# Two-block network in one kernel: in block 1 both row tiles of the third attention are finished ahead of the fourth's, with output products between them

## The chip, the cores and the metric

The kernel runs on one core of a Trainium2 chip. The metric is the device time of one execution in microseconds (us), as the median of several runs. TensorE (PE) does matrix products and transposes, VectorE (DVE) and ScalarE (ACT) work on the elements, GpSimd (POOL) does a few powers, SyncE (SP) issues the loads of the weights.

## The reference

Two different blocks of two layers each work on 256 rows of 1024 columns in float32. The change is in block 1. One of its layers, cut to what matters:

```
def hybrid_layer(x, ...):                       # x: 256 rows x 1024
    proj = rmsnorm(x, g_pre_mix) @ w_in         # all inputs of four attentions
    o_a = dsa_attention(...)                    # columns   0..255 of mix
    o_b = forgetting_attention(...)             # columns 256..511
    o_c = differential_attention(...)           # columns 512..767: softmax(q1 k1) - lam * softmax(q2 k2),
                                                #   times v, then an rmsnorm over each head
    o_d = sliding_window_sink_attention(...)    # columns 768..1023
    mix = jnp.concatenate([o_a, o_b, o_c, o_d], axis=-1)
    x = x + rmsnorm(mix @ w_out, g_post_mix)    # the output product
    m = jnp.square(jax.nn.relu(rmsnorm(x, g_pre_mlp) @ w_up)) @ w_down
    x = x + rmsnorm(m, g_post_mlp)
    return x + jax.nn.sigmoid(x @ w_ple_gate) * (p_i @ w_ple_proj)
```

Each attention has four heads of 64 columns, and all are causal. The differential attention has two softmaxes per head, so eight in a row tile.

## The kernel before, in words

The 256 rows are two row tiles of 128, t = 0 and 1. Row 0's tile sees 128 keys, tile 1 sees 256, so tile 1's attention is about twice the work. A float32 product is done as three products of rounded halves (hi and lo), for accuracy.

`layer1` writes one layer of block 1. The projections come first. The attentions are generators (`att_a`, `att_b`, `differ` for the third, `att_d` for the fourth; one per row tile for the last two, `gen_c` and `gen_d`) that are put in the list `self.side`. Long runs of products call `tick` after every few matmuls; a tick advances the first two generators of the list by one step. `until` and `drain` tick on until the named generators, or all, are done. Thus the work of the attentions is written between the products. A scheduler then orders the instructions of each engine, near the order in which they are written; each engine runs its own list in order and waits at the head of it.

One softmax goes through four engines (`soft`, `pv`): PE makes the scores of a head (line 386), DVE adds the mask and takes the maximum (387), ACT takes the exponential with its sum (398); for the third attention DVE divides by the sums and subtracts (555 to 560); PE transposes the result (411), ACT copies it from the bank (413), PE multiplies by the values (419). The third attention ends with its norm: ACT copies and squares (568, 569), DVE sums (571), POOL takes the power (225), DVE scales twice (573, 574).

The output product `mix @ w_out` needs `mix` transposed: `transpose_in` transposes columns of one row tile (249) and splits them into hi and lo (ACT 230, DVE 231) in `mT`. `mT` has eight k-tiles of 128 columns: 0 to 3 are the first two attentions, 4 and 5 the third, 6 and 7 the fourth. `mm_pair` (284) then does, per row tile and k-tile, three terms for each half of the 1024 output columns, six matmuls of 512 columns; 96 in a layer. `pss[t]` are the banks in which they add up. `norm(t)` then squares them (347), scales (798 to 802) and transposes the outcome (249) for the MLP, whose first products are line 268 and, from line 325 on, the wide ones.

Before the change the list is sorted so that tile 0 of the third and of the fourth attention go first, side by side, and then tile 1 of both. The columns 512 to 1023 of a tile are transposed at once, four k-tiles in a row.

Of the kernel before, what the change touches and what calls it, by code (L numbers as in the profile page):

```python
# [21 lines left out]
NT = S // P  # L22
# [107 lines left out]
class Net:  # L130
# [448 lines left out]
    def layer1(self, i, xT):  # L579
# [47 lines left out]
        def q_alone(q, rows=64):  # L627

            qT = [wk.tile([P, 2, 2, P], F32, name="qT", tag="qT") for _ in range(64 // rows)]
            self.tr_alone(lambda r: qT[r // 2][:, r % 2], q, 2, rows)  # L630
            return qT
# [10 lines left out]
        mix = [wk.tile([P, D], F32, name="mix", tag="mix") for _ in range(NT)]  # L642
# [89 lines left out]
        mT = self.new_parts(KT)  # L732
# [8 lines left out]
        gen_c = [self.differ(i, t, lambda t: q_alone(cq[t], 32), kTc, vc, mix[t]) for t in range(NT)]  # L741
# [14 lines left out]
        get = self.w.rows(a["w_out"][i], 0, KT)  # L756
        pss = [[self.bank(self.acc) for _ in range(2)] for _ in range(NT)]
# [5 lines left out]
        def att_d(t):  # L763
            yield from self.attend(t, qTd, kTd, vd, lambda h: h // 2, lambda h: self.window[:, S - (t + 1) * P:],
                                   mix[t][:, 768:1024], self.sink[:, i, :])

        gen_d = [att_d(t) for t in range(NT)]
# [5 lines left out]
        gboth = self.row(a["norm_post_mix"][i])  # L773
        self.pin(nc.vector.tensor_tensor(gboth, gboth, gmlp, op=ALU.mult))
        self.transpose_in(mix[1][:, :512], mT, 1, 4)
        self.side.sort(key=lambda gen: gen in (gen_c[1], gen_d[1]))
        self.mm_pair(pss[0], mT, 0, range(1, 4), get, start=False, stop=False)
        self.until(gen_c[0], gen_d[0])
        self.transpose_in(mix[0][:, 512:], mT, 0, 4, 4)
        self.mm_pair(pss[0], mT, 0, range(4, 6), get, start=False, stop=False)  # L780
        self.mm_pair(pss[1], mT, 1, range(2), get, stop=False)
        self.mm_pair(pss[0], mT, 0, range(6, 8), get, start=False, apart=2)
        xg = []

# [8 lines left out]
        def norm(t):  # L793
            ss = self.square_sum(pss[t])
            u = wk.tile([P, D], F32, name="u", tag="w4")
            for j in range(2):
                sl = slice(j * 512, (j + 1) * 512)
                nc.vector.tensor_tensor(u[:, sl], pss[t][j], gboth[:, sl], op=ALU.mult)
            r = self.rsqrt(self.total(ss), 1.0 / D, EPS)
            for j in range(2):  # L800
                sl = slice(j * 512, (j + 1) * 512)
                nc.vector.scalar_tensor_tensor(xg[t][:, sl], u[:, sl], r, xg[t][:, sl], op0=ALU.mult, op1=ALU.add)
                self.transpose_in(xg[t][:, sl], hT, t, 4, 4 * j)
            us[t], rs[t] = u, r
# [7 lines left out]
            self.pin(nc.vector.tensor_tensor(X[t], X[t], u, op=ALU.add))  # L812

        us, rs = [None] * NT, [None] * NT
        self.mm_pair(pss[1], mT, 1, range(2, 4), get, start=False, stop=False)
        self.drain()
        self.transpose_in(mix[1][:, 512:], mT, 1, 4, 4)
        self.mm_pair(pss[1], mT, 1, range(4, 6), get, start=False, stop=False)
        norm(0)
        self.mm_pair(pss[1], mT, 1, range(6, 8), get, start=False, apart=2)  # L820
        gain(1)
        gpost = self.row(a["norm_post_mix"][i])
# [51 lines left out]
        for f in range(NG - 2):  # L874
            cur = up(f + 1)
            get = self.w.rows(a["w_mlp_down"][i], f * 4, 4)
# [13 lines left out]
        get = self.w.rows(a["w_mlp_down"][i], 4 * NG - 8, 8)  # L890
# [33 lines left out]
        get = self.w.rows(a["w_ple_gate"][i], 0, KT)  # L924
# [4 lines left out]
        pss = [[self.bank(self.acc) for _ in range(2)] for _ in range(NT)]  # L929
# [572 lines left out]
```

## Time and profile before

| what | value |
|---|---|
| median of 3 runs | 1939.16 us (1939.14 to 1940.99) |
| the profiled execution's own time | 1937.16 us |
| its span in the trace | 1935.4 us |
| mean granted TensorE clock | 0.988 of full speed |
| PE busy | 1877.3 us, 97% of the span |
| DVE busy | 1306.8 us, 68% |
| ACT busy | 1035.9 us, 54% |

A matmul in the trace has its modelled end, which overlaps the next one's start; how long one holds PE is read from start to start. Float32 products that aren't split in hi and lo (scores, products with the values) stand as two records each. The granted clock is 1.00 at 2.4 GHz and 0.50 at 1.2 GHz. A row of the windows gives the stretch, its length, the busy time (and instructions) of PE, of its weight loads, of DVE, ACT and POOL, then the granted clock, the busy share of the DMA engines and GB/s.

### The profile page before, as it was taken

The page shows a single profiled execution, that of the slowest core. Times are in us where ns is not written, and L with a number is a line of the kernel's source. Part 1 is how long each engine was busy: PE and PEld are TensorE (multiplying, and loading weights), DVE is VectorE, ACT ScalarE, POOL GpSimd, SP SyncE. Part 2 cuts the span into 40 slices and gives each one's busy share as a digit, 9 for nine tenths or more (in the row PEclk, how much of TensorE's full clock was granted, in tenths as well). Part 3 has the DMA queues.
Part 4 walks back from the last instruction along what each step waited for, and adds up shares of the span by engine and source line. Part 5 has one row for each costly group of instructions (what it writes and reads, how often), then busy time and mean ns, then how long its engine had stood idle before and what let it go on. Part 6 is the DMA issues. An engine that isn't in the chain of part 4 may idle for free.

```text
span 1935.4 us, 27780 instructions
## 1 busy us (share of the span) xinstructions
PE 1877.3 (97%) x10282; PEld 1614.0 (83%) x10282; DVE 1306.8 (68%) x2456; ACT 1035.9 (54%) x1743; POOL 77.8 (4%) x127
## 2 busy tenths in 40 slices
PE   7898999999989999999999999999999999999997
PEld 6787878887878888888888988887988888988886
DVE  6866756687776666558666667566558666677555
ACT  5555544564654545566555655554565555655552
POOL 2000000000000000100000000000000000000000
PEclk9998999999999999999999999999999999999999
DMA  7433676554335555655555656664454555656662
GB/s 214 131 112 97 209 241 210 164 179 133 110 123 186 180 203 158 188 162 162 176 179 181 221 174 211 195 186 141 155 170 155 182 182 172 206 168 217 186 193 89
DMA packets 187132, 334.00 MB, mean 173 GB/s; under 512 B 11622, under 2 KB 109078, under 8 KB 186612
## 3 DMA queue, kind: packets, MB, share of 16 engines
q1 hardware_dynamic: 180160, 308.94, 50.4%
q0 software_dynamic: 6528, 23.18, 3.9%
q8 instruction: 81, 1.33, 0.3%
q14 instruction: 55, 0.45, 0.1%
q10 hardware_dynamic: 308, 0.10, 0.0%
HBM read 331.10 MB, written 4.62 MB: 173 GB/s over the span
## 4 chain that ended last, share of the span: by engine, by line
PE 83%; DVE 7%; DMA 4%; ACT 4%; issue 2%; POOL 0%; DVEq 0%; SPq 0%; ACTq 0%; POOLq 0%
PE bank L325 23%; PE bank L284 20%; PE bank L268 13%; PE bank L327 12%; DMA wraw<-in_w_in_dram 3%; DVE wlo L103 2%; PE bank L386 2%; PE bank L419 2%; PE bank L315 2%; PE bank L314 2%; PE bank L313 2%; ACT whi L102 1%; PE bank L249 1%; ACT pr L398 1%; PE bank L411 1%
## 5 line engine op out<-in xcount | busy, mean ns | idle before, releaser
L103 DVE TENSOR_TENSOR wlo<-wraw,whi 128x1024 fp32r<-128x1024 f32 (+1 forms) x628 | 711.0, 1147 | 328.7 <-ACT whi L102 238.6
L102 ACT ACTIVATE whi<-wraw 128x1024 fp32r<-128x1024 f32 (+1 forms) x628 | 608.9, 997 | 346.1 <-PE bank L284 110.2
L325 PE MATMUL bank<-phl,whi 128*128 128x512 f32 x2080 | 532.3, 395 | 0.4 <-ACT whi L102 0.4
L325 PEld LDWEIGHTS bank<-phl,whi 128*128 128x128 f32 x2080 | 374.9, 189 | 69.1 <-ACT whi L102 1.2
L284 PE MATMUL bank<-whi,phl 128*128 128x512 f32 x1280 | 358.2, 395 | 1.7 <-ACT phl L230 1.0
L268 PE MATMUL bank<-whi,phl 128*128 128x512 f32 (+4 forms) x1152 | 341.2, 378 | 4.3 <-ACT whi L102 2.2
L327 PEld LDWEIGHTS bank<-phl,wlo 128*128 128x128 f32 x2080 | 284.2, 190 | 23.2 <-DVE wlo L103 2.7
L327 PE MATMUL bank<-phl,wlo 128*128 128x256 f32 x2080 | 291.8, 283 | 0.6 <-DVE wlo L103 0.6
L284 PEld LDWEIGHTS bank<-whi,phl 128*128 128x128 f32 x1280 | 237.4, 189 | 53.3 <-ACT phl L230 2.9
L268 PEld LDWEIGHTS bank<-whi,phl 128*128 128x128 f32 x1152 | 210.9, 191 | 34.9 <-ACT phl L230 3.8
L268 PE MATMUL bank<-wlo,phl 128*128 128x512 f32 (+4 forms) x576 | 215.4, 376 | 2.4 <-DVE wlo L103 2.3
L284 PE MATMUL bank<-wlo,phl 128*128 128x512 f32 x640 | 206.2, 394 | 0.1
L284 PEld LDWEIGHTS bank<-wlo,phl 128*128 128x128 f32 x640 | 120.2, 188 | 28.8 <-DVE wlo L103 2.8
L268 PEld LDWEIGHTS bank<-wlo,phl 128*128 128x128 f32 x576 | 110.0, 191 | 18.2 <-DVE wlo L103 4.3
L315 PE MATMUL bank<-phl,wlo 128*128 128x256 f32 x304 | 86.3, 284 | 0.0
L314 PE MATMUL bank<-phl,whi 128*128 128x256 f32 x304 | 86.1, 283 | 0.0
L225 POOL TENSOR_TENSOR ry<-ry,mhalf 128x1 f32<-128x1 f32 (+1 forms) x40 | 32.9, 824 | 1309.1 <-DVE ry L224 1301.6
L313 PE MATMUL bank<-phl,whi 128*128 128x256 f32 x304 | 85.5, 281 | 0.0
L313 PEld LDWEIGHTS bank<-phl,whi 128*128 128x128 f32 x304 | 57.7, 190 | 0.2
L314 PEld LDWEIGHTS bank<-phl,whi 128*128 128x128 f32 x304 | 57.3, 189 | 0.2
L315 PEld LDWEIGHTS bank<-phl,wlo 128*128 128x128 f32 x304 | 57.5, 189 | 0.0
L230 ACT ACTIVATE phl<-bank 128x512 fp32r<-128x512 f32 (+2 forms) x60 | 32.8, 571 | 44.0 <-PE bank L249 43.6
(301 smaller groups left out, 1720.9 us busy)
## 6 DMA issues: line engine op xcount, KB each, us to landing
wraw<-in_w_in_dram SPq DMA_DIRECT2D x172, 512.0 KB, 4.6
wraw<-in_w_mlp_up_dram SPq DMA_DIRECT2D x64, 512.0 KB, 4.6
wraw<-in_w_mlp_down_dram SPq DMA_DIRECT2D x64, 512.0 KB, 4.5
wraw<-in_w_ffn_gate_dram SPq DMA_DIRECT2D x44, 512.0 KB, 4.7
wraw<-in_w_ffn_up_dram SPq DMA_DIRECT2D x44, 512.0 KB, 4.5
wraw<-in_w_ffn_down_dram SPq DMA_DIRECT2D x44, 512.0 KB, 4.4
wraw<-in_w_in_dram SPq DMA_DIRECT2D x54, 384.0 KB, 3.8
wraw<-in_w_out_dram SPq DMA_DIRECT2D x32, 512.0 KB, 4.3
```

The costliest lines, as they stand in the source:

```text
L102: first = nc.scalar.activation(hi[:, :n], src, AF.Copy)
L103: ins = nc.vector.tensor_tensor(lo[:, :n], src, hi[:, :n].bitcast(F32), op=ALU.subtract)
L225: nc.gpsimd.tensor_tensor(y, y, self.mhalf[:, :n], op=ALU.pow)
L268: self.order(nc.tensor.matmul(ps, self.part(parts, kt)[x][:, sl], get(kt + kbase)[w], start=start and n == 0, stop=stop and n == len(terms ...
L284: ins = nc.tensor.matmul(pss[j], self.part(parts, kt)[x][:, sl], get(kt + kbase)[w][:, j * 512:(j + 1) * 512], start=start and n == 0, sto ...
L313: self.order(nc.tensor.matmul(ps, wh, xh, start=first, stop=False, **kw), n == 0)
L314: nc.tensor.matmul(ps, wh, xl, start=False, stop=False, **kw)
L315: nc.tensor.matmul(ps, wl, xh, start=False, stop=last, **kw)
L325: self.order(nc.tensor.matmul(flat, get(kt)[0][:, c:c + P], both, start=n == 0, stop=False), n == 0)
L327: nc.tensor.matmul(ps[:, 0], get(kt)[1][:, c:c + P], self.part(parts, kt)[0], start=False, stop=n == len(kts) - 1)
L386: nc.tensor.matmul(o, qs(h), ks(h), start=True, stop=True)
L419: nc.tensor.matmul(po[:, h * 64:(h + 1) * 64], pts[kb][:, h, :], v(kb, h), start=kb == 0, stop=kb == t)
```

## The change

In `layer1`, the sort of the list is left out, so the third attention's two tiles are advanced together first, and the fourth's after them. The transposes into `mT` go by two k-tiles: the third attention's for both row tiles once both are done, then the fourth's for tile 0, then for tile 1. The products of k-tiles 0 and 1 of tile 1 are written ahead of the wait for the third attention, those of 4 and 5 of tile 0 and of 2 and 3 of tile 1 behind it. `norm(0)` is written ahead of tile 1's last four k-tiles.

```
-        self.side.sort(key=lambda gen: gen in (gen_c[1], gen_d[1]))
         self.mm_pair(pss[0], mT, 0, range(1, 4), get, start=False, stop=False)
-        self.until(gen_c[0], gen_d[0])
-        self.transpose_in(mix[0][:, 512:], mT, 0, 4, 4)
+        self.mm_pair(pss[1], mT, 1, range(2), get, stop=False)
+        self.until(*gen_c)
+        for t in range(NT):
+            self.transpose_in(mix[t][:, 512:768], mT, t, 2, 4)
         self.mm_pair(pss[0], mT, 0, range(4, 6), get, start=False, stop=False)
-        self.mm_pair(pss[1], mT, 1, range(2), get, stop=False)
+        self.mm_pair(pss[1], mT, 1, range(2, 4), get, start=False, stop=False)
+        self.until(gen_d[0])
+        self.transpose_in(mix[0][:, 768:], mT, 0, 2, 6)
         self.mm_pair(pss[0], mT, 0, range(6, 8), get, start=False, apart=2)
...
-        self.mm_pair(pss[1], mT, 1, range(2, 4), get, start=False, stop=False)
+        norm(0)
+        self.mm_pair(pss[1], mT, 1, range(4, 6), get, start=False, stop=False)
         self.drain()
-        self.transpose_in(mix[1][:, 512:], mT, 1, 4, 4)
-        self.mm_pair(pss[1], mT, 1, range(4, 6), get, start=False, stop=False)
-        norm(0)
+        self.transpose_in(mix[1][:, 768:], mT, 1, 2, 6)
         self.mm_pair(pss[1], mT, 1, range(6, 8), get, start=False, apart=2)
```

The lists of the built programs show where this puts the work. In the names below, `bank_1460` and `bank_1461` are `pss[0]`, `bank_1462` and `bank_1463` are `pss[1]`; `phl_1024` holds k-tiles 0 to 3 of `mT`, `phl_1025` k-tiles 4 to 7; `mix_165` and `mix_166` are the two row tiles of `mix`. All is in layer 0; layer 1 has the same pattern.

On PE, before, the products of tile 0 with k-tiles 4 to 7 stand among the scores of tile 1 of the third (`kT_1168`) and of the fourth attention (`kT_1470`):

```order
L386 MATMUL bank_1635<-kT_1168,qT_1569 128x256
L284 MATMUL bank_1460<-whi_1438,phl_1025 128x512
L284 MATMUL bank_1461<-whi_1438,phl_1025 128x512
L386 MATMUL bank_1640<-kT_1168,qT_1569 128x256
L386 MATMUL bank_1654<-kT_1470,qT_1481 128x256
L284 MATMUL bank_1460<-whi_1438,phl_1025 128x512
L284 MATMUL bank_1461<-whi_1438,phl_1025 128x512
```

With the change, the first product of k-tiles 4 to 7 on PE stands behind the values' products of tile 1 of the third attention (`pt_1662`) and behind the transposes of the fourth attention's tile 1 (`pr_1667`):

```order
L419 MATMUL bank_1688<-v_1166,pt_1662 128x64
L411 MATMUL bank_1708<-ident_79,pr_1667 128x128
L411 MATMUL bank_1715<-ident_79,pr_1667 128x128
L249 MATMUL bank_1722<-ident_79,mix_165 128x128 x2
L411 MATMUL bank_1708<-ident_79,pr_1667 128x128
L411 MATMUL bank_1715<-ident_79,pr_1667 128x128
L411 MATMUL bank_1708<-ident_79,pr_1667 128x128
L411 MATMUL bank_1715<-ident_79,pr_1667 128x128
L411 MATMUL bank_1708<-ident_79,pr_1667 128x128
L411 MATMUL bank_1715<-ident_79,pr_1667 128x128
L284 MATMUL bank_1460<-whi_1438,phl_1025 128x512
L284 MATMUL bank_1461<-whi_1438,phl_1025 128x512
```

So no output product is left between the scores of tile 1 and this place; the last one ahead of it is of k-tile 3 of tile 1.

The second place is where PE transposes what `norm(0)` made (`xg_1765` before, `xg_1785` now), ahead of the last products of tile 1. Before, the transposes of `mix_166` stand first, and 24 products of `pss[1]` behind:

```order
L419 MATMUL bank_1745<-v_1166,pt_1725 128x64
L249 MATMUL bank_1781<-ident_79,mix_166 128x128 x4
L249 MATMUL bank_1814<-ident_79,xg_1765 128x128 x4
L249 MATMUL bank_1822<-ident_79,xg_1765 128x128 x2
L284 MATMUL bank_1462<-whi_1438,phl_1025 128x512
L284 MATMUL bank_1463<-whi_1438,phl_1025 128x512
```

With the change, five products of `pss[1]` stand between the last product of `pss[0]` (`bank_1461`) and these transposes:

```order
L284 MATMUL bank_1461<-wlo_1457,phl_1025 128x512
L284 MATMUL bank_1463<-whi_1444,phl_1025 128x512
L284 MATMUL bank_1462<-whi_1444,phl_1025 128x512
L284 MATMUL bank_1463<-whi_1444,phl_1025 128x512
L284 MATMUL bank_1462<-wlo_1445,phl_1025 128x512
L284 MATMUL bank_1463<-wlo_1445,phl_1025 128x512
L249 MATMUL bank_1803<-ident_79,xg_1785 128x128 x4
L249 MATMUL bank_1811<-ident_79,xg_1785 128x128 x4
L249 MATMUL bank_1830<-ident_79,mix_166 128x128 x2
```

Here twelve of the products of tile 1 with k-tiles 4 to 7 have gone ahead of the transposes, and the other twelve stay behind them.

On ACT, the end of the third attention's tile 1 (`oc_1697`, `ocs_1698`) now has the fourth's exponentials (`pr_1667`) inside it:

```order
L413 ACTIVATE pt_1662<-bank_1657 128x512
L568 ACTIVATE oc_1697<-bank_1688 128x256
L395 ACTIVATE es_1679<-es_1679 128x4
L398 ACTIVATE pr_1667,sm_1664<-pr_1667,nm_1665 128x256 x4
L569 ACTIVATE ocs_1698<-bank_1688 128x256
L230 ACTIVATE phl_1025<-bank_1722 128x2x128
```

Before, these exponentials stand ahead of the third attention's last copies (`pt_1725`), and `oc` and `ocs` follow each other:

```order
L398 ACTIVATE pr_1653,sm_1650<-pr_1653,nm_1651 128x256 x4
L347 ACTIVATE sq_1803,ss_1800<-bank_1461 128x512
L413 ACTIVATE pt_1698<-bank_1693 128x512
L413 ACTIVATE pt_1705<-bank_1700 128x512
L413 ACTIVATE pt_1718<-bank_1713 128x512
L413 ACTIVATE pt_1725<-bank_1720 128x512
L568 ACTIVATE oc_1754<-bank_1745 128x256
L569 ACTIVATE ocs_1755<-bank_1745 128x256
```

`bank_1722`, split in the last row shown of the change, holds tile 0's columns of the third attention.

## Rows read from the trace of the kernel before

**Rows 1.** The page, part 4: shares of the span by engine, chain that ended last.

```profile
PE 83%; DVE 7%; DMA 4%; ACT 4%; issue 2%; POOL 0%; DVEq 0%; SPq 0%; ACTq 0%; POOLq 0%
```

**Rows 2.** Windows from a layer's first output product to line 325, layers 0 and 1.

```profile
130.36:195.02 64.66, 57.27 (x293) 47.15 (x291) 46.51 (x121) 35.86 (x86) 5.55 (x8) 0.92 0.35 112
510.73:573.94 63.21, 55.75 (x292) 45.58 (x291) 46.52 (x121) 35.84 (x86) 5.02 (x7) 0.95 0.35 114
```

**Rows 3.** Timeline of PE, layer 0: start, us, instructions [idle before <- releaser].

```profile
128.60 1.89 PE L419 MATMUL bank<-v,pt 128*128 128x64 f32 x16
...
145.93 0.27 PE L411 MATMUL bank<-ident,pr 128*128 128x128 f32 x1
...
151.07 0.74 PE L284 MATMUL bank<-whi,phl 128*128 128x512 f32 x2 [0.25 <-ACT phl L230]
...
153.44 1.08 PE L284 MATMUL bank<-whi,phl 128*128 128x512 f32 x4
154.36 0.63 PE L284 MATMUL bank<-wlo,phl 128*128 128x512 f32 x2
154.82 1.89 PE L386 MATMUL bank<-kT,qT 128*128 128x256 f32 x8
156.36 0.81 PE L284 MATMUL bank<-whi,phl 128*128 128x512 f32 x2
...
159.30 0.58 PE L284 MATMUL bank<-wlo,phl 128*128 128x512 f32 x1
...
166.78 3.73 PE L419 MATMUL bank<-v,pt 128*128 128x64 f32 x16 [0.52 <-ACT pt L413]
173.93 1.12 PE L249 MATMUL bank<-ident,mix 128*128 128x128 f32 x4 [3.42 <-DVE mix L574]
```

**Rows 4.** Timeline of PE, layer 1, the piece like the one at 166.78.

```profile
547.15 2.37 PE L419 MATMUL bank<-v,pt 128*128 128x64 f32 x16 [0.52 <-ACT pt L413]
```

**Rows 5.** Windows around the change of the granted clock, layers 0 and 1.

```profile
164.00:166.90 2.90, 2.33 (x17) 2.06 (x18) 2.16 (x6) 1.20 (x3) 0.54 (x1) 1.00 0.00 0
166.90:173.90 7.00, 3.61 (x16) 3.38 (x16) 1.44 (x4) 0.97 (x3) 1.02 (x1) 0.50 0.00 0
173.93:177.19 3.26, 3.26 (x15) 2.96 (x15) 2.11 (x3) 1.19 (x2) 0.58 (x1) 0.51 0.00 0
549.20:556.00 6.80, 3.38 (x15) 2.89 (x15) 3.35 (x7) 1.85 (x4) 1.40 (x2) 0.50 0.00 0
```

**Rows 6.** DVE by line and form, 130.36 to 195.02: xcount | busy, mean ns.

```profile
L103 DVE TENSOR_TENSOR wlo<-wraw,whi 128x1024 fp32r<-128x1024 f32 x13 | 15.5, 1218 | 2.7 <-ACT whi L102 2.6
L387 DVE CUSTOM_DVE_ANT_0 pr<-bank,c_causal 128x256 f32<-128x256 f32 x8 | 3.2, 421 | 0.1
L560 DVE SCALAR_TENSOR_TENSOR df<-pr,rsum 128x256 f32<-128x256 f32 x4 | 1.8, 478 | 0.0
L558 DVE TENSOR_SCALAR pr<-pr,rsum 128x256 f32<-128x256 f32 x4 | 1.2, 348 | 0.0
```

**Rows 7.** ACT by line and form, the same stretch.

```profile
L413 ACT ACTIVATE pt<-bank 128x512 f32<-128x512 f32 x6 | 3.3, 588 | 2.1 <-PE bank L419 1.7 <-PE bank L411 0.4
L398 ACT ACTIVATE pr<-pr,nm 128x128 f32<-128x128 f32 x4 | 1.6, 390 | 0.0
L568 ACT ACTIVATE oc<-bank 128x256 f32<-128x256 f32 x2 | 0.8, 384 | 3.6 <-PE bank L419 3.6
```

**Rows 8.** The chain that ended last, in order of time, layer 0: start, us, what.

```profile
158.81 1.97 ACT pr L398 x8
...
162.89 0.58 ACT sq L347 x2
...
163.50 0.69 DVE u L798
...
164.53 0.54 POOL ry L225
...
171.95 1.02 POOL ry L225
```

## The prediction

> **What bounds the kernel now.** I read the chain that ended last first: PE has 83% of it [rows 1]. So a microsecond counts if PE waits in it, or runs at the lower clock; DVE and ACT count only where PE waits for them. Then I read the stretch that the change touches, from the first output product to line 325, once per layer: 64.66 us in layer 0, 63.21 us in layer 1 [rows 2]. PE is busy 57.27 and 55.75 us of them, so it waits about 7.4 us in each. The timeline shows the longest of these waits: 3.42 us ahead of the transposes at 173.93, until the third attention's tile 1 has its norm [rows 3]. The windows show that PE runs there at 1.2 GHz: 0.50 from 166.9 to 173.9 and 0.51 to 177.19 [rows 5]. Layer 1 has the same work, and its clock falls later, at 549.2 [rows 5]: sixteen records of products with the values take 2.37 us there [rows 4] and 3.73 us in layer 0 [rows 3]. This 1.36 us is nearly the whole difference of 1.45 us between the layers, so what PE loses there by its clock goes onto the path.
>
> What fills PE between 145.93 and that end matters most. At 145.93 the 48 products of k-tiles 0 to 3 are done in both tiles. From 151.07 to 159.30 stand the 24 products of tile 0 with k-tiles 4 to 7, between the scores of both attentions [rows 3]. They cover the softmaxes of tile 1, which are work of DVE and ACT.
>
> **What the change moves.** No matmul is added or removed. Two splits of 512 columns become four of 256, some tenths of a microsecond on ACT and DVE, which have room (36 and 47 us busy of 64) [rows 2]; I cost them at nothing. POOL issues a row of gains some 6 us later; it is needed only in the MLP. The order of PE is what counts. Up to k-tile 3 it holds the same products, so I start the walk at 145.9 as before. From there to the first product of k-tile 4 the new list holds only scores, transposes and products with the values, though tile 0's columns of the third attention are there at 151.07 at the latest, where before multiplies them [rows 3]. That stretch lasts as long as the chain of the third attention's tile 1 and then the fourth's, at full clock:
>
> DVE takes nine maxima, six of 256 columns at 0.42 [rows 6]: 2.6 us. Four exponentials of the first softmax: 2.0 [rows 8]. ACT then does the fourth attention's tile 0, four at 0.39 and a copy of 0.59 [rows 7], with about 0.9 of waiting for PE's transposes between: 3.1. Four exponentials of the second softmax: 2.0. Dividing and subtracting, two at 0.35 and two at 0.48 [rows 6] and small ones: 1.9. Six transposes and two copies: 1.7. The products with the values, 16 records at 0.11 (1.89 us for 16 [rows 3]), and a score product between: 2.0. Then ACT's copy `oc`, 0.38 [rows 7], and four exponentials of the fourth's tile 1: 2.6 with the small one. The last transposes and the split of tile 0: 0.7. The sum is 18.6 us, so the first product leaves at 164.5 instead of 151.07. PE has about 8.8 us to do in it: nine score products of two records at 0.19 (eight records from 154.82 to 156.36 [rows 3]), 3.4; 22 transposes at 0.11, half of the 0.22 at the lower clock (four in 1.12 us with the last one's end [rows 3]), 2.4; 24 records of the values, 2.6; the two narrow scores, 0.4. It waits the other 9.8 us.
>
> From 164.5 PE still has 96 products of 512 columns (48 of line 284, 48 of line 268) at 0.23 (four in 153.44 to 154.36 [rows 3]), 22.1 us; 16 records, 1.8; 26 transposes, 2.9: 26.8 us. It waits for the third attention's norm about 0.9 us (POOL's 1.02 [rows 8] is in it) with seven products as cover. It waits for `norm(0)`: from the squares at 162.89 to POOL's start at 164.53 are 1.64 us, POOL 0.54 [rows 8], a scaling of 512 columns 0.7 like the 0.69 at 163.50 [rows 8]; that is 2.9 us with five products, 1.1 us, as cover, and DVE's list now has a weight's subtraction of 1.2 [rows 6] there, of which some 0.7 shows: 2.5 us. 0.6 us of small waits stay. So line 325 is reached at 164.5 + 26.8 + 4.0 = 195.3, and the stretch takes 64.9 us at full clock. Against the trace that is 2 x 64.9 - (64.66 + 63.21) = +1.9 us: the walk alone is about even, since before has its clock loss in it and the walk none.
>
> **The clock.** In layer 0 of before it fell at 166.9 [rows 5], 7.6 us after the last product of 512 columns at 159.30 [rows 3]; in between PE was 2.33 us busy in the 2.90 us from 164.0 [rows 5], with records of 64 columns, and it still fell. It came back at about 177.2, soon after products had started again [rows 5]. The new stretch without such products is 18.6 us long and emptier, so I expect 1.2 GHz from about 153.5, 7.6 us behind 145.9, to 165.7, 1.2 us into the products. PE's work in it is 6.4 us at full rate: eight score records 1.5, 18 transposes 2.0, 16 records 1.8, five products 1.1. Bounds of the price: 0, if PE's waits swallow it all, and 6.4 if nothing does. By the nearest row, the 16 records above, what others wait for goes through whole: those records 1.8, a score product 0.4, eight transposes 0.9 and the first products 1.1. I take 4.2 us a layer.
>
> The Trainium skill, "TensorE: Matmul & The Clock Gate", section "Why this matters for your kernels", puts mid-kernel losses of the clock down to long idle gaps between bursts of matmuls. By that rule the change would keep its clock, since its longest wait is shorter than the 3.42 us of before; the sum would be +1.9 us. The trace disagrees so far: the fall at 166.9 came ahead of the 3.42 us wait.
>
> **Sum.** 64.9 + 4.2 = 69.1 a layer; +4.4 in layer 0, +5.9 in layer 1, +10.3 us. The profiled execution's 1937.16 us becomes 1947.5; the median of the runs shown is 2.0 us above that execution, so I forecast **1949.5 us**. Nothing later gives it back: PE is the path behind the stretch.
>
> **Rivals.**
> - The clock stays at 2.4 GHz. PE is never idle for as long as before. Against it: the fall in rows 5. It gives 1939.16 + 1.9 = 1941.1 us, no change that can be measured. The rule of the page named above is this rival.
> - A second fall: the 2.5 us wait for `norm(0)` brings the lower clock again, over some 16 products; about 2 us more a layer, 1953.5 us. For it: it is the longest single wait of the walk. Against it: a dense run of products stands right ahead of it.
> - Faster: the two softmax chains overlap instead of adding up. ACT alone has about 11 us of work in the 18.6 us (12 wide exponentials 5.9, four narrow 1.6, three copies 1.6, a weight part 1, small ones 1). The tail's 3.42 us wait is gone in any case. A stretch of 14 us with the clock kept gives 4.6 us less a layer than the walk: 1941.1 - 9.2 = 1931.9 us. It decides from 15.7 us down (0.2% is 3.9 us, 2.9 a layer below the walk); with the clock loss, from 11.5. Against it: ACT's list has the exponentials of the fourth's tile 1 behind `oc`, in order.
>
> That the change doesn't do what it says can be left out: the lists of the engines show it.
>
> **How the numbers follow.** Forecast 0.72 (its own range 1945 to 1953, from half to nearly the whole of the 6.4 us); second fall 0.12; clock kept 0.10; overlap 0.04; something between clock kept and forecast 0.02. 0.2%, 3.9 us, is about what a measurement of this kernel can tell from no change: faster 0.04, same 0.10, slower 0.86. The range from 1943.5 to 1955.5 leaves out the kept clock, the overlap and the upper part of the second fall.
>
> **What would show it.** In the profile after, PE's timeline should have no line 284 between about 146 and 164 to 169 in layer 0; its waits there should sum to some 7 to 10 us, for ACT and DVE; the clock should be 0.50 over several microseconds from 150 to 157 on; transposes of `xg` should wait 2 to 3 us; the stretch to line 325 should take 68 to 71 us in each layer, and the 3.42 us wait for `mix` should be gone. I am wrong if the clock stays at 1.00 in that stretch, or if the first product of k-tile 4 leaves before 160.

## The result and the profile after

The changed kernel takes 1949.05 us (median of 4 runs, 1948.17 to 1950.09) against 1939.15 us (4 runs, 1935.06 to 1940.99) of the kernel before on the same chip: ratio 1.0061, 95% interval 1.0045 to 1.0076 (the medians alone give 1.0051). It is slower by 9.9 us; 1949.5 was forecast, between 1943.5 and 1955.5. The profiled execution took 1948.17 us, its span is 1946.3 us and its mean granted clock 0.982.

Line numbers of `layer1` behind the edit are 2 or 3 higher than before; those of the helpers are the same.

The page, part 4 (beside [rows 1]): PE's share of the chain that ended last.

```profile
PE 87%; DVE 7%; ACT 2%; DMA 2%; issue 1%; POOL 0%; ACTq 0%; DVEq 0%; SPq 0%; POOLq 0%
```

Windows of the changed kernel from a layer's first output product to line 325 (beside [rows 2]).

```profile
128.24:198.00 69.76, 62.47 (x292) 49.15 (x291) 46.20 (x123) 36.37 (x88) 5.57 (x8) 0.88 0.32 103
512.99:584.21 71.22, 63.46 (x292) 51.13 (x291) 46.32 (x123) 36.39 (x88) 6.08 (x7) 0.86 0.32 101
```

The stretch is 5.10 us longer in layer 0 and 8.01 us in layer 1, 13.1 us together, with the granted clock at 0.88 and 0.86 in the mean. DVE and ACT have as much work as before (46.20 us for 46.51, 36.37 for 35.86). That the whole is only 9.9 us slower is no gain elsewhere that the change made: the first product starts at 128.24, where it was 130.36, though nothing ahead of it was edited. In the ten other profiles of this study that start lies anywhere from 128.60 to 132.49.

Timeline of PE in the changed kernel, layer 0, from the first scores of 256 columns to the MLP (beside [rows 3]).

```profile
139.29 2.10 PE L386 MATMUL bank<-kT,qT 128*128 128x256 f32 x10
141.15 1.17 PE L284 MATMUL bank<-whi,phl 128*128 128x512 f32 x4
...
143.55 0.61 PE L284 MATMUL bank<-wlo,phl 128*128 128x512 f32 x2
144.16 2.44 PE L386 MATMUL bank<-kT,qT 128*128 128x256 f32 x12
147.13 0.70 PE L386 MATMUL bank<-kT,qT 128*128 128x256 f32 x2 [0.53 <-DVE mx L387]
148.95 1.60 PE L411 MATMUL bank<-ident,pr 128*128 128x128 f32 x4 [1.12 <-ACT pr L398]
151.24 1.97 PE L419 MATMUL bank<-v,pt 128*128 128x64 f32 x8 [0.69 <-ACT pt L413]
...
155.01 1.22 PE L386 MATMUL bank<-kT,qT 128*128 128x256 f32 x2 [0.53 <-DVE mx L387]
...
162.85 0.44 PE L411 MATMUL bank<-ident,pr 128*128 128x128 f32 x2 [1.05 <-ACT pr L398]
...
164.85 2.08 PE L284 MATMUL bank<-whi,phl 128*128 128x512 f32 x4
...
179.44 1.29 PE L249 MATMUL bank<-ident,xg 128*128 128x128 f32 x8 [2.72 <-DVE xg L805]
...
181.24 0.63 PE L268 MATMUL bank<-wlo,phl 128*128 128x512 f32 x1
181.67 0.63 PE L268 MATMUL bank<-whi,phl 128*128 128x512 f32 x1
```

Layer 1, the same places.

```profile
528.91 2.44 PE L386 MATMUL bank<-kT,qT 128*128 128x256 f32 x12
...
550.66 2.06 PE L284 MATMUL bank<-whi,phl 128*128 128x512 f32 x4
...
565.70 1.55 PE L249 MATMUL bank<-ident,xg 128*128 128x128 f32 x8 [3.25 <-DVE xg L805]
```

From 144.16 to 164.85 PE has no output product, only the scores, transposes and products with the values of the two attentions: 20.69 us, and 21.75 us in layer 1 (528.91 to 550.66). Before there were two such holes, from 145.93 to 151.07 and, behind the product at 159.30, past the transposes at 173.93 [rows 3], up to the next product:

```profile
175.98 1.20 PE L284 MATMUL bank<-whi,phl 128*128 128x512 f32 x2
```

The two are 5.1 and 16.7 us long, so before was not without products for a shorter time. What the change loses shows beside a kernel with its order and with cover (e1 below, 12.25 us). The wait of 3.42 us for `mix` [rows 3] is gone; a wait for `xg` of 2.72 and 3.25 us has come.

Windows of the changed kernel: the stretch without output products, then the stretches at the lower clock in layer 0, then in layer 1 (beside [rows 5]).

```profile
144.16:164.85 20.69, 16.51 (x69) 11.77 (x68) 11.95 (x56) 11.10 (x42) 0.00 (x0) 0.73 0.25 81
150.20:160.40 10.20, 8.95 (x31) 6.63 (x31) 4.49 (x18) 3.64 (x11) 0.00 (x0) 0.50 0.26 87
...
163.80:167.20 3.40, 3.37 (x10) 2.44 (x11) 1.70 (x7) 2.09 (x6) 1.01 (x1) 0.50 0.00 0
180.90:184.30 3.40, 3.40 (x10) 2.62 (x10) 2.65 (x4) 0.74 (x2) 0.46 (x1) 0.50 0.20 73
...
535.90:553.00 17.10, 15.48 (x56) 12.78 (x57) 6.20 (x27) 7.01 (x24) 1.01 (x1) 0.50 0.11 36
566.60:570.00 3.40, 3.40 (x12) 2.85 (x11) 2.78 (x4) 1.24 (x3) 0.00 (x0) 0.50 0.19 74
```

PE runs at 1.2 GHz in the hole, and a second time behind the wait for `xg`.

### The profile page after: what moved, and what is told of

Read it like the earlier page. It is cut to its first block, busy times and chain, and to the rows that moved or that the text cites. A ratio compares the mean times of both kernels' runs of the same rounds, so it can differ in the third digit from the quotient of the medians.

```text
span 1946.3 us, 27797 instructions
## 1 busy us (share of the span) xinstructions
PE 1888.7 (97%) x10282; PEld 1621.0 (83%) x10282; DVE 1306.5 (67%) x2460; ACT 1037.9 (53%) x1747; POOL 78.9 (4%) x127
## 4 chain that ended last, share of the span: by engine, by line
PE 87%; DVE 7%; ACT 2%; DMA 2%; issue 1%; POOL 0%; ACTq 0%; DVEq 0%; SPq 0%; POOLq 0%
PE bank L325 23%; PE bank L284 21%; PE bank L268 14%; PE bank L327 12%; PE bank L419 3%; PE bank L386 3%; DVE wlo L103 2%; PE bank L315 2%; PE bank L314 2%; PE bank L313 2%; DMA wraw<-in_w_in_dram 2%; PE bank L411 1%; PE bank L249 1%; PE bank L1257 1%; ACT whi L102 1%
```

## The experiments

Nine kernels were run, in three sets, each beside the kernel before: 1937.71 us for e1 to e4 (15 runs), 1938.06 for e5 to e7 (12 runs), 1937.15 for e8 and e9 (17 runs). The three sets ran on three chips, so a difference in microseconds between kernels of different sets carries that of the chips; the ratios to before don't. All but e6 and e7 are edits of the changed kernel. "Stretch" is that of the first windows above, "hole" the time from the start of the last row of products of k-tiles 0 to 3 to that of the next products, layer 0 (21.30 us in the changed kernel; in e3 two more k-tiles of products stand ahead of it).

| kernel | median us (range, runs) | ratio to before [95%] | stretch, layers 0, 1 | hole |
|---|---|---|---|---|
| e1_hold | 1938.12 (1933.5 to 1941.11, 11) | 1.0003 [0.9994, 1.0012] | 64.01, 63.90 | 12.25 |
| e2_sort | 1945.36 (1944.6 to 1948.67, 5) | 1.0042 [1.0030, 1.0055] | 67.77, 69.40 | 21.38 |
| e3_early | 1953.05 (1951.49 to 1954.18, 4) | 1.0078 [1.0064, 1.0092] | 71.68, 70.61 | 21.19 |
| e4_normlate | 1944.93 (1941.72 to 1945.6, 5) | 1.0032 [1.0020, 1.0045] | 66.10, 66.63 | 20.40 |
| e5_warm | 1946.84 (1944.82 to 1950.24, 5) | 1.0050 [1.0035, 1.0066] | 68.76, 70.73 | 21.00 |
| e6_order_only | 1932.56 (1930.89 to 1933.4, 8) | 0.9970 [0.9960, 0.9981] | 60.84, 60.81 | 11.89 |
| e7_order_pieces | 1931.29 (1928.23 to 1932.75, 5) | 0.9964 [0.9950, 0.9979] | 59.80, 59.79 | 11.48 |
| e8_hold_and_late | 1932.71 (1931.34 to 1936.1, 11) | 0.9979 [0.9971, 0.9988] | 61.77, 61.16 | 12.24 |
| e9_warm_more | 1948.69 (1942.62 to 1951.87, 6) | 1.0054 [1.0038, 1.0070] | 66.66, 68.21 | 19.91 |

**e1_hold.** Two k-tiles of tile 1's products are written behind the wait for the third attention, not ahead of it.

```diff
         self.mm_pair(pss[0], mT, 0, range(1, 4), get, start=False, stop=False)
-        self.mm_pair(pss[1], mT, 1, range(2), get, stop=False)
         self.until(*gen_c)
...
         self.mm_pair(pss[0], mT, 0, range(4, 6), get, start=False, stop=False)
+        self.mm_pair(pss[1], mT, 1, range(2), get, stop=False)
```

> The change, with the first products of tile 1 (k-tiles 0 and 1) written behind the wait for the third attention instead of ahead of it; PE's list then has 22 products of tile 1 among the first scores of the third attention's tile 1. Theory A (the change loses because PE has no product of 512 columns left under the softmax chains of the third and fourth attention): those 22 products, 5.0 us, go under the chain, the half-rate stretch shrinks, and the stretch from first output product to line 325 falls from some 70 us to 61 to 64 in each layer; about 14 us less than the change, 1932 to 1938 us, not slower than before. Theory B (the order of the attentions costs, third wholly ahead of fourth, as its chains then stand in series): the order is the same, so 1949 us within 2. Theory C (the early norm(0) costs): unchanged as well, 1949 us.

The whole loss is gone; 1938.12 us is 0.1 us above theory A's range. Windows of e1_hold over the two stretches, and its PE timeline in layer 0:

```profile
131.12:195.13 64.01, 56.84 (x292) 46.40 (x291) 45.99 (x123) 36.25 (x88) 6.57 (x8) 0.95 0.35 113
510.24:574.14 63.90, 56.72 (x292) 46.42 (x291) 46.02 (x123) 36.27 (x88) 5.97 (x7) 0.95 0.34 113
```

```profile
139.58 2.64 PE L386 MATMUL bank<-kT,qT 128*128 128x256 f32 x12
141.87 0.58 PE L284 MATMUL bank<-whi,phl 128*128 128x512 f32 x1
...
147.56 0.71 PE L284 MATMUL bank<-whi,phl 128*128 128x512 f32 x2
148.11 0.27 PE L411 MATMUL bank<-ident,pr 128*128 128x128 f32 x1
...
150.50 0.61 PE L284 MATMUL bank<-wlo,phl 128*128 128x512 f32 x2
152.24 1.10 PE L419 MATMUL bank<-v,pt 128*128 128x64 f32 x8 [1.12 <-ACT pt L413]
...
162.75 1.65 PE L284 MATMUL bank<-whi,phl 128*128 128x512 f32 x5
```

PE's list holds the same instructions. In the change ten records of scores stand at 139.29, twelve products follow from 141.15 on, and only then, at 144.16, the next twelve records of scores. In e1_hold twelve stand at 139.58, the rest among the products, and 24 products stand between those first scores and the hole (141.87 to 150.50), while DVE and ACT do the softmaxes. ACT's timelines, of the changed kernel and then of e1_hold, show the first exponential of that tile:

```profile
146.09 0.51 ACT L398 ACTIVATE pr<-pr,nm 128x256 f32<-128x256 f32 x1 [1.29 <-DVE nm L390]
```

```profile
143.77 0.51 ACT L398 ACTIVATE pr<-pr,nm 128x256 f32<-128x256 f32 x1 [3.14 <-DVE nm L390]
```

That is 17.85 us behind the first output product (128.24) in the changed kernel and 12.65 us (131.12) in e1_hold. The chain of softmaxes starts 5.2 us earlier, and the hole is 9.05 us shorter. From this exponential to the first product behind the hole it is 18.76 us in the changed kernel (to 164.85) and 18.98 in e1_hold (to 162.75): the chain is no shorter, it starts sooner and has more products beside it.

PE's list is not all that moved. In the changed kernel DVE has two weight splits and a row of gains in its list, 3.4 us, between the first maximum (139.93) and the second:

```profile
140.28 2.36 DVE L103 TENSOR_TENSOR wlo<-wraw,whi 128x1024 fp32r<-128x1024 f32 x2
142.55 1.22 DVE L774 TENSOR_TENSOR row<-row 128x1024 f32<-128x1024 f32 x1
143.68 0.42 DVE L387 CUSTOM_DVE_ANT_0 pr<-bank,c_causal 128x256 f32<-128x256 f32 x1
```

In e1_hold they don't stand there. How much of the 5.2 us is DVE's list, and how much the scores that PE reaches only at 144.16, was not tried.

**e2_sort.** The sort of the list is put back; all else stays changed.

```diff
         self.transpose_in(mix[1][:, :512], mT, 1, 4)
+        self.side.sort(key=lambda gen: gen in (gen_c[1], gen_d[1]))
         self.mm_pair(pss[0], mT, 0, range(1, 4), get, start=False, stop=False)
```

> The change, with the sort of the list put back, so that tile 0 of the third and of the fourth attention go first again. Theory A: the first product of k-tile 4 still stands behind the chain of the third attention's tile 1, since the transposes of k-tiles 4 and 5 wait for both tiles; the stretches stay at 67 to 70 us, 1945 to 1949 us in all. Theory B (order of the attentions): the order is that of before, so it goes back to 1939 us within 2. Theory C: 1949 us.

3.7 us below the change, with intervals that overlap, and still clearly above before: the order of the attentions is not what costs. The hole is as long as in the change. One wait stands in it that the change does not have; PE timeline of e2_sort:

```profile
156.99 2.17 PE L411 MATMUL bank<-ident,pr 128*128 128x128 f32 x8 [3.75 <-ACT pr L398]
```

**e3_early.** The wait for the third attention goes tile by tile, so that tile 0's products of k-tiles 4 and 5 can start before tile 1 has ended.

```diff
-        self.until(*gen_c)
-        for t in range(NT):
-            self.transpose_in(mix[t][:, 512:768], mT, t, 2, 4)
+        self.until(gen_c[0])
+        self.transpose_in(mix[0][:, 512:768], mT, 0, 2, 4)
         self.mm_pair(pss[0], mT, 0, range(4, 6), get, start=False, stop=False)
         self.mm_pair(pss[1], mT, 1, range(2, 4), get, start=False, stop=False)
+        self.until(gen_c[1])
+        self.transpose_in(mix[1][:, 512:768], mT, 1, 2, 4)
```

> The change, with tile 0's columns of the third attention transposed and multiplied as soon as tile 0 is done, ahead of the wait for tile 1: 12 products (2.7 us) come forward, to the scores of tile 1. Theory D (what the prediction put first: these products stand behind both chains, and the stretch is as long as the chain): PE gets 2.7 us of cover, and some of the half rate goes: 3 to 5 us a layer less, 1940 to 1943 us. Theory A in its narrow form (cover counts only where the chain doesn't wait for PE): the 12 products go ahead of scores that the chain needs, push it back by as much, and nothing is won: 1947 to 1951 us.

Neither range held: it is the slowest by its median. PE timeline of e3_early:

```profile
149.63 1.17 PE L284 MATMUL bank<-whi,phl 128*128 128x512 f32 x4
...
152.03 0.62 PE L284 MATMUL bank<-wlo,phl 128*128 128x512 f32 x2
152.49 1.82 PE L386 MATMUL bank<-kT,qT 128*128 128x256 f32 x6
...
170.31 1.12 PE L249 MATMUL bank<-ident,mix 128*128 128x128 f32 x4 [2.50 <-DVE mix L574]
...
174.92 2.91 PE L284 MATMUL bank<-whi,phl 128*128 128x512 f32 x6
```

The twelve products do come early, at 149.63 to 152.49, and the scores at 152.49 stand behind them. But the chain is no later for it. ACT's copy `oc` of the third attention's outcome, in e3_early and then in the changed kernel:

```profile
164.97 0.39 ACT L568 ACTIVATE oc<-bank 128x256 f32<-128x256 f32 x1 [0.94 <-PE bank L419]
```

```profile
161.83 0.38 ACT L568 ACTIVATE oc<-bank 128x256 f32<-128x256 f32 x1 [3.05 <-PE bank L419]
```

That is 32.51 us behind the first output product (132.46) in e3_early and 33.59 (128.24) in the change. The twelve products are missed behind it: the transposes of `mix` at 170.31 wait 2.50 us for the third attention's norm, where in the change the products from 164.85 on stand and no such wait shows. So the hole stays 21.19 us long, with twelve products fewer left to follow it, and six of those run at 1.2 GHz (in 2.71 us, to 177.63). Nothing is won, as the narrow form of theory A had it, but not because the chain is pushed back. That e3 is slower than the change is not shown: the intervals overlap, and its stretches are 1.92 us longer and 0.61 shorter.

**e4_normlate.** `norm(0)` goes back behind tile 1's last transposes.

```diff
         us, rs = [None] * NT, [None] * NT
-        norm(0)
         self.mm_pair(pss[1], mT, 1, range(4, 6), get, start=False, stop=False)
         self.drain()
         self.transpose_in(mix[1][:, 768:], mT, 1, 2, 6)
+        norm(0)
```

> The change, with norm(0) back behind the last transposes of mix: 12 more products of tile 1 stand between the last product of tile 0 and the transposes of xg. Theory C (the early norm(0) is the cost): the wait of 2.72 and 3.25 us before these transposes goes and the short fall of the clock behind it (at about 181 and 567) with it, and nearly all of the 10 us comes back: 1940 us. Theory A: the wait shrinks to about 1 us and the short fall goes, 1.5 to 3 us a layer: 1943 to 1946 us; the empty stretch ahead stays.

Some 4 us of the 9.9, as theory A said; the two intervals just touch. The profile is of one of its two shorter runs (1941.72 and 1942.4 us, mean clock 0.989 and 0.988); the others took 1944.93 to 1945.6 at 0.984 and 0.985. The transposes of `xg` in e4_normlate's PE timeline:

```profile
184.35 1.29 PE L249 MATMUL bank<-ident,xg 128*128 128x128 f32 x8 [0.15 <-DVE xg L805]
```

The wait is 0.15 us, and no lower clock follows it. From the first product behind the hole to line 325 it takes 30.41 us in both layers (168.18 to 198.59, 549.46 to 579.87), where the change takes 33.15 (164.85 to 198.00) and 33.55.

**e5_warm and e9_warm_more.** Useless products of 512 columns go into the bank of each group of transposes (line 411) in the stretch, ahead of the transposes that overwrite it: three a group in e5, five in e9. `self.fill` is set only in the stretch.

```diff
-            ps = self.bank()
+            ps = self.warm(self.bank())
...
+    def warm(self, ps, n=3):
+        if self.fill:
+            for _ in range(n):
+                self.nc.tensor.matmul(ps, *self.fill, start=True, stop=True)
+        return ps
```

> The change, with work added: from the third k-tile products on until both attentions are done, three products of 512 columns without use go into each bank ahead of the transposes of a softmax (lines 411), five banks a layer, 15 products or 3.4 us of PE at full rate a layer; the transposes overwrite them. They wait for no softmax, so PE does them where it would idle. Theory A with its clock term (PE waits some 9 us in the stretch, and the half rate costs 4 to 6 us a layer on top): the clock stays at 1.00 for most of 146 to 165 and the stretch falls from 70 to 71 us to 65 to 68: 1941 to 1946 us, although PE has more to do. Rival (the half rate lies in PE's waits and costs nothing, all the loss is the chain): no gain, 1949 us or up to 4 us more.

> As e5_warm, but five useless products of 512 columns ahead of each group of transposes in the stretch, 25 a layer, instead of three; they are extra work, 5.8 us a layer at 0.23 each, and their outcome is overwritten. Theory A (the lower clock costs something of its own in the stretch, 1 to 3 us a layer): if the clock holds, the stretch without output products shortens from the 21.3 and 22.4 us of the change to 19 to 20; 1943 to 1947 us. Rival (PE's time in the stretch is all hidden behind the softmaxes): the stretch stays at 21 to 22 us whatever the clock; 1947 to 1950. If the added products get into the path: above 1950.

e5 doesn't decide: its interval overlaps that of the change. Its profile is of its longest run, 1950.24 us at a mean clock of 0.986, and there the clock still fell in the hole; three others took 1944.82 to 1946.84 at 0.989 or 0.990, and no profile shows where they had it. e9 does decide by its profile, though its median doesn't: three of its runs took 1942.62 to 1945.93 at a mean clock of 0.990 or 0.991, three 1951.46 to 1951.87 at 0.988. The profiled one, 1942.62, kept the clock. Windows of e9_warm_more: the stretches of both layers, then the hole of layer 0.

```profile
130.63:197.29 66.66, 60.40 (x318) 48.73 (x316) 46.49 (x123) 36.41 (x88) 5.57 (x8) 1.00 0.34 108
512.20:580.41 68.21, 61.48 (x317) 50.08 (x316) 46.58 (x123) 36.41 (x88) 6.07 (x7) 0.97 0.33 105
146.56:165.85 19.29, 16.87 (x93) 13.37 (x94) 12.42 (x57) 12.19 (x43) 0.84 (x1) 1.00 0.25 84
```

With 25 products more, the stretch is 3.10 us shorter than that of the change in layer 0 and 3.01 in layer 1. So the lower clock costs at least 3 us a layer; at least, since some of the added products may lengthen the path, and layer 1 still has a second fall. The three runs at 0.988 took 5.5 to 9.3 us more than the other three. If what they lack is the clock in these two stretches, which no profile of them shows, that is 2.8 to 4.6 us a layer.

**e6_order_only and e7_order_pieces.** Here the kernel before is edited. e6 takes only the order from the change: the sort goes, and both tiles of the third attention are waited for, then the fourth's tile 0.

```diff
-        self.side.sort(key=lambda gen: gen in (gen_c[1], gen_d[1]))
         self.mm_pair(pss[0], mT, 0, range(1, 4), get, start=False, stop=False)
-        self.until(gen_c[0], gen_d[0])
+        self.until(*gen_c)
+        self.until(gen_d[0])
```

e7 is e6 with tile 1's last columns transposed in two pieces, the third attention's ahead of `drain`:

```diff
-        self.drain()
-        self.transpose_in(mix[1][:, 512:], mT, 1, 4, 4)
+        self.transpose_in(mix[1][:, 512:768], mT, 1, 2, 4)
         self.mm_pair(pss[1], mT, 1, range(4, 6), get, start=False, stop=False)
+        self.drain()
+        self.transpose_in(mix[1][:, 768:], mT, 1, 2, 6)
```

> The kernel before, with nothing changed but the order of the attentions: no sort, and the wait of its first until split into the third attention's two tiles and then the fourth's tile 0. The transposes stay at four k-tiles and the products where they were written, all of tile 1's behind the wait. Theory A: the order as such costs nothing; 22 products of tile 1 lie under the chain, tile 1 of the third is done some 10 us earlier, so the 3.42 us wait and its half rate go: 2 to 4 us a layer less than before, 1931 to 1935 us. Theory B (this order puts the chains in series): slower than before, 1943 us or more.

> The run before this one, and tile 1's transposes by two k-tiles as in the change: the third attention's columns of tile 1 are transposed ahead of the drain, its products of k-tiles 4 and 5 run while the fourth attention's tile 1 ends, and norm(0) comes behind. Theory A: 12 more products cover the end of the fourth attention and the wait for norm(0), about 1 us a layer more: 1929 to 1933 us, the fastest. Theory E (pieces of two k-tiles cost, by more splits and banks): 1 to 2 us slower than the run before this one.

Both are faster than before. e7 has the lowest median of all, and its stretch is 1.0 us shorter than e6's in both layers, as theory A said, though the intervals of the two overlap. Windows of e7_order_pieces:

```profile
130.96:190.76 59.80, 55.59 (x292) 44.95 (x291) 45.32 (x122) 36.19 (x87) 5.57 (x8) 0.97 0.38 120
507.30:567.09 59.79, 55.52 (x292) 45.18 (x291) 45.32 (x122) 36.28 (x87) 5.03 (x7) 0.97 0.38 121
```

**e8_hold_and_late.** The edits of e1 and e4 together, on the changed kernel.

> Both undone at once: tile 1's products of k-tiles 0 and 1 stand behind the wait for the third attention, as in e1_hold, and norm(0) stands behind tile 1's last transposes, as in e4_normlate; left of the change are the order of the attentions and the transposes by two k-tiles. Theory A (two separate prices, the lost cover and the early norm): the gains of e1_hold (11 us below the change) and of e4_normlate (4 us) add up; 1932 to 1936 us, the stretch without output products 12 us, no wait over 1 us for xg. Rival B (they share one price, so the second is free once the first is gone): 1937 to 1940, as e1_hold.

1932.71 us, where e6 is. So the two prices are separate: 10.9 us less with e1, 4.1 with e4, 16.3 with both (15.0 would be the sum); by the ratios 0.58, 0.29 and 0.82% (0.87). What is left of the change (the order, and transposes by two k-tiles) is a gain on the kernel before of 0.21%.

## Why the prediction was right, step by step

**The lost cover.** Shown by e1: moving products back among the softmaxes takes the loss away. The reason given for it was narrower than the truth. The prediction looked only at tile 0's products of k-tiles 4 to 7 and took the list up to k-tile 3 as unchanged; but the products of those k-tiles could be cover too, and the change used them up ahead of the chain: the last twelve stand ahead of all scores but the ten records at 139.29. That no output product is left between the scores of tile 1 and the hole, as it is put where the change is described, holds for the scores from 144.16 on. e3 adds that products brought forward leave another wait open, there the one for the third attention's norm. What part DVE's list has in e1's gain is open.

**The length of the hole.** Forecast were 18.6 us at full clock plus the 3.1 of the clock's 4.2 that lie in it; measured are 20.69 and 21.75. At full clock it is 19.29 with e9's products in it. The rest was forecast at 30.8 and 1.1 for the clock, 31.9; it takes 33.15 and 33.55. With the 15.92 us ahead of the hole (128.24 to 144.16, 15.57 before), that makes 69.76, against 69.1.

**Two terms were off, in opposite ways.** The walk at full clock was forecast at 64.9 us; the stretch that ran wholly at full clock (e9, layer 0) takes 66.66. The clock was forecast at 4.2 us; e9 gives 3.1 and 3.0, so the walk was some 1.8 too short and the clock about 1.1 too dear, if e9's products cost nothing. If they do, the clock is dearer than that, and by the split of e9's runs 4.2 may be right; this stays open. Inside the walk, PE's waits in the hole were put at 9.8 us (7 to 10 where it says what would show it): PE was busy 16.51 of 20.69 us and idle 4.18. Its records at 1.2 GHz fill much of what would have been waits: at full clock, in e9, it was busy 16.87 of 19.29 us, and some 5.8 of that, an estimate from 25 at 0.23, were the added products. The stretch of layer 1, 71.22 us, is a little above the 68 to 71 that were to show.

**Where the clock fell.** Forecast was 153.5 to 165.7, measured are 150.20 to 160.40 and again 163.80 to 167.20; in layer 1 it is one piece, 535.90 to 553.00. PE's longest wait ahead of the first fall is the 1.12 us at 148.95, so the rival with the clock kept is out. The Trainium skill, "TensorE: Matmul & The Clock Gate", section "Why this matters for your kernels", puts such losses down to long idle gaps; the trace disagrees for this fall, as it did before. The second fall does come behind a long wait, 2.72 us in layer 0. But in layer 0 of e9 the same wait stands with no fall behind it, the clock being 1.00 over the whole stretch:

```profile
180.28 1.29 PE L249 MATMUL bank<-ident,xg 128*128 128x128 f32 x8 [2.72 <-DVE xg L806]
```

The Trainium skill, the same page, section "Terms", puts the price of a lower clock at about the throttled time times the share of pulses left out. By that, an estimate, the 17.0 us at 0.50 in layer 0 (10.20 + 3.40 + 3.40) would cost 8.5; e9 shows about 3 by its profile and at most 4.6 by the split of its runs, and in the hole PE waits for others anyway.

**The wait for `norm(0)`.** 2.5 us were forecast, 2.72 and 3.25 are measured. The second fall, a rival with 0.12, came too, in both layers: at 181.24 and 181.67 products follow each other in 0.43 us, not 0.23, for the 3.40 us at 0.50, in which PE is never idle, so that half of it (1.7) is lost. So the likeliest case and this rival happened together; by e9's profile the first clock loss was smaller than forecast (20.69 us of hole for 19.29, so 1.4 for 3.1) and hid it. The forecast wait for the third attention's norm, 0.9, does not show in the change's timeline.

**The faster rival.** The chains do not overlap in the changed kernel: the fourth attention's exponentials stand behind `oc` (161.83 above). Nor do they in e1. ACT's timelines, the changed kernel and then e1_hold:

```profile
162.21 0.50 ACT L398 ACTIVATE pr<-pr,nm 128x256 f32<-128x256 f32 x1
```

```profile
157.60 0.39 ACT L568 ACTIVATE oc<-bank 128x256 f32<-128x256 f32 x1 [1.86 <-PE bank L419]
...
159.39 0.51 ACT L398 ACTIVATE pr<-pr,nm 128x256 f32<-128x256 f32 x1
```

The holes of 11.48 to 12.25 us (e1, e6 to e8) are below the 14 us that this rival supposed, and e6 to e8 take 1931 to 1933 us, near its 1931.9, but by cover and not by overlap.

**The total.** +10.3 us was forecast from the stretches; they gave +13.1 in the profiled execution, 2.1 of it made up by the earlier start. That the forecast of the median is within 0.5 us is partly luck. Why the start varies was not tried.

## What to carry to other kernels

Independent matmuls cover a chain through other engines only if they stand in PE's list behind the instructions that start the chain and ahead of those that end it; before moving a block of them, write down which chain stays without cover, and look at what the other engines' lists do with the move. Here the same instructions in another place made 11 us (e1), and twelve products brought forward won nothing, as they were missed at the next wait (e3). Waiting for both tiles in the order in which they are needed was a gain of 0.3% once the cover stayed where it was, so an edit with several parts is worth taking apart before it is dropped.

## What the runs showed of the hardware

In e9 25 useless products of 512 columns a layer made the stretch of layer 0 shorter, 66.66 us for 69.76, with the clock at 1.00, that is 2.4 GHz, in the profiled run; with 15 of them it still fell in the profiled run of e5. The same e9 ran at a mean clock of 0.988 in three of six runs, 5.5 to 9.3 us longer than the other three. The time from the span's start to the first output product, with the same code, varied from 128.24 to 132.49 us between profiled executions.
